# Weight differences of an fp32 encoder's MLPs by adding DMA transfers

## The chip, the cores and the metric

The kernel runs on one core of a Trainium2 chip. The metric is device time in microseconds (us); the median of three runs is compared. A core has TensorE (PE, with its weight loads as PEld), VectorE (DVE), ScalarE (ACT), GpSimd (POOL) and SyncE (SP), and 16 DMA engines that move data between HBM and SBUF.

## The reference

A two-layer encoder on x of shape (1, 512, 1024), all in float32. Layer 0 mixes tokens by dilated sliding-window attention, layer 1 by latent attention; each mixer is followed by an MLP with 4096 hidden columns:

```python
def sq_relu_mlp(h, w1, w2):
    a = jax.nn.relu(h @ w1)
    return (a * a) @ w2

def reference(x, ...):
    for i in range(DEPTH):
        h = rms_norm(x, norm_mix[i])
        ...
        x = x + y
        h = rms_norm(x, norm_ffn[i])
        x = x + sq_relu_mlp(h, ffn_w1[i], ffn_w2[i])
    return x
```

The change lies in the two MLPs alone.

## The kernel before

**Three passes for float32.** TensorE multiplies in the rounded format float32r. Each operand is split into a high part (its rounding) and a low part (the rest), and a product is summed from high x high, high x low and low x high. A weight unit is a tile of 128 partitions x 2 x 512 values (512 KB). `load_unit` brings it into `raw` by a DMA that SP issues, ScalarE copies it to `whi` (rounding it), and VectorE forms `wlo = raw - whi`. There are three buffers of `raw` and four each of `whi` and `wlo`, shared by everything that splits weights.

**The first matmul** (`up`) works in chunks of 1024 hidden columns, each in two groups of 512. A group has four units; each unit feeds 24 matmuls (2 slices of k, 4 output tiles `acc`, 3 passes). Then ScalarE evacuates each `acc` with a ReLU and squares it. The first group of a layer is special: it takes all four units at once and goes over the tokens in two halves.

**The second matmul** (`wino`, called by `down`) multiplies each chunk's 1024 x 1024 weight block with seven products of quarter blocks instead of eight, in the order 1, 5, 6, 3, 7, 2, 4. Each of the four quarters (b11, b12, b22, b21) is two units in `wqs`, loaded by SP. Some products need a difference of quarters: b11 is overwritten with b12 - b11 for product 5, then with b22 minus that for product 6, then with b21 minus that for product 4; b12 becomes b22 - b12 for product 7. `sub` does it, in two halves, on VectorE. Then `split_w` makes the high and low part as above, and 12 matmuls (PE tiles `sc` and `tp`) use each unit. VectorE also forms sums of activations (`stmp`) and adds the results to the residual stream (`add_to`). The last chunk of a layer goes another way (`down_last`).

**Order.** A layer runs up(0,0), up(0,1), then for each of three chunks up(ch+1,0), down(ch), up(ch+1,1), and down_last(3). Each engine has one instruction queue in fixed order, which a scheduler lays out when the program is built. Buffers come free by semaphores when their last reader is done.

Of the kernel before, what the change touches and what calls it, by code (L numbers as in the profile page):

```python
# [10 lines left out]
F32 = mybir.dt.float32  # L11
F32R = mybir.dt.float32r
AF = mybir.ActivationFunctionType
ALU = mybir.AluOpType
# [5 lines left out]
NT = S // P  # L20
# [67 lines left out]
def encoder_kernel(ctx: ExitStack, tc: tile.TileContext, x, norm_mix, norm_ffn, a_w_qkv, a_q_gain, a_k_gain,  # L88
                   a_w_o, b_w_in, b_q_a_gain, b_w_qb, b_kv_a_gain, b_w_kvb, b_q_gain, b_k_gain, b_w_o,
                   ffn_w1, ffn_w2, consts, out):  # L90
    nc = tc.nc
    V, A, G, PE = nc.vector, nc.scalar, nc.gpsimd, nc.tensor
    uid = [0]

    def nm(s):
        uid[0] += 1
        return f"{s}_{uid[0]}"
# [50 lines left out]
            nc.sync.dma_start(dst, src)  # L148
        return raw

    def load_unit(src, nk, dims, n, key=None, home=None):

        raw = early.pop(key) if key in early else load_raw(src, nk, dims, n)
        if home is None:
            home = [wp.tile([P, 2, 512], F32R, tag=t, name=nm(t)) for t in ("whi", "wlo")]
        hi, lo = home
        A.activation(hi[:, :nk, :n], raw[:, :nk, :n], AF.Copy)  # L157
        V.tensor_tensor(lo[:, :nk, :n], raw[:, :nk, :n], hi[:, :nk, :n].bitcast(F32), op=ALU.subtract)  # L158
        return hi, lo, nk

    def run_block(units, groups, n, mm, evac, outs=NT, name=None, halves=1):

        accs = [acc_p.tile([P, 512], F32, tag="acc", name=nm("acc")) for _ in range(outs)]
        total = sum(u[1] for u in units)
        ui = 0
        kt0 = 0  # L170
        for gi, g in enumerate(groups):
            loaded = []
            for _ in range(g):
                src, nk, dims = units[ui]
                loaded.append(load_unit(src, nk, dims, n, (name, ui)))
                ui += 1
            nkt = 0
            for hv in range(halves):
                for o in range(outs):
                    kt = kt0  # L180
                    for hi, lo, nk in loaded:
                        for j in range(nk):
                            for p_i, (lt, rt, oc) in enumerate(mm(o, kt, hi[:, j], lo[:, j], hv)):
                                PE.matmul(accs[o][:, oc], lhsT=lt, rhs=rt, start=(kt == 0 and p_i == 0 and hv == 0),  # L184
                                          stop=(kt == total - 1 and p_i == 2), skip_group_check=halves > 1)
# [303 lines left out]
    def wino(tag, Aq, w, wqs, pool, resid):  # L489

        v = w.rearrange("(k p) c -> p k c", p=P)
        raw, S = {}, {}

        def load(key, slot):
            ki, ni = key  # L500
            raw[key] = []
            for u in range(2):
                t = wqs[:, 2 * slot + u]
                k0 = 4 * ki + 2 * u
                nc.sync.dma_start(t, v[:, k0:k0 + 2, 512 * ni:512 * ni + 512])
                raw[key].append(t)
        for key, slot in zip(((0, 0), (0, 1), (1, 1), (1, 0)), SLOTS[tag % 2]):
            load(key, slot)
        b11, b12, b22, b21 = raw[0, 0], raw[0, 1], raw[1, 1], raw[1, 0]

        def sub(o, x, y):
            for u in range(2):
                V.tensor_tensor(o[u], x[u], y[u], op=ALU.subtract)  # L513

        def stmp(name, x, y, op):
            if name not in S:
                S[name] = pool.tile([P, 4, 256], F32, tag="S", name=nm("S"), bufs=2)
            V.tensor_tensor(S[name], x, y, op=op)

        def split_w(x):  # L520
            hi = wp.tile([P, 2, 512], F32R, tag="whi", name=nm("whi"))
            lo = wp.tile([P, 2, 512], F32R, tag="wlo", name=nm("wlo"))
            A.activation(hi, x, AF.Copy)  # L523
            V.tensor_tensor(lo, x, hi.bitcast(F32), op=ALU.subtract)  # L524
            return hi, lo

        def operands(p):
            if p == 1:
                return Aq(0, 0), b11
            if p == 5:  # L530
                stmp("c", Aq(1, 0), Aq(1, 1), ALU.add)
                sub(b11, b12, b11)
                return S["c"], b11
            if p == 6:
                stmp("c", S["c"], Aq(0, 0), ALU.subtract)
                sub(b11, b22, b11)
                return S["c"], b11
            if p == 3:
                stmp("c", Aq(0, 1), S["c"], ALU.subtract)
                return S["c"], b22  # L540
            if p == 7:
                stmp("d", Aq(0, 0), Aq(1, 0), ALU.subtract)
                sub(b12, b22, b12)
                return S["d"], b12
            if p == 2:
                return Aq(0, 1), b21
            sub(b11, b21, b11)
            return Aq(1, 1), b11

        def add_to(i, n, banks):  # L550
            for t in range(2):
                sl = resid[:, 2 * i + t, 512 * n:512 * n + 512]
                V.tensor_tensor(sl, sl, banks[t], op=ALU.add)

        banks = {}
        for p, chain, first, adds in ORDER:
            a, wq = operands(p)
            at = split_a(a, pool)
            if first:
                pl, tg = (sc_p, "sc") if chain == "a" else (tp_p, "tp")  # L560
                banks[chain] = [pl.tile([P, 512], F32, tag=tg, name=nm(tg)) for _ in range(2)]
            bk = banks[chain]
            for u in range(2):
                hi, lo = split_w(wq[u])
                for t in range(2):
                    for j in range(2):
                        k = 2 * u + j
                        ah = at[:, k, 0, t * P:(t + 1) * P]
                        al = at[:, k, 1, t * P:(t + 1) * P]
                        for i, (lt, rt) in enumerate(((ah, hi), (ah, lo), (al, hi))):  # L570
                            PE.matmul(bk[t], lhsT=lt, rhs=rt[:, j], start=(first and k == 0 and i == 0),  # L571
                                      stop=(k == 3 and i == 2), skip_group_check=True)
            for i, n in adds:
                add_to(i, n, bk)
# [6 lines left out]
    def mlp(layer, w1, w2, hT_m, resid, pool, done):  # L581
# [4 lines left out]
        def up(ch, grp):  # L586
# [6 lines left out]
            c0 = ch * 1024 + grp * 512  # L593
            first = c0 == 0
# [9 lines left out]
                A.activation(a2[:, f], acc, AF.Relu)  # L604
# [351 lines left out]
```

## Time and profile before

| | us |
|---|---|
| runs shown (3): lowest, median, highest | 1454.57, 1455.29, 1456.9 |
| profiled execution: its own time | 1457.98 |
| profiled execution: span | 1456.2 |
| PE busy in the span | 1422.8 |
| DVE busy | 903.5 |
| ACT busy | 710.3 |
| POOL busy | 117.4 |

A busy time is the sum of an engine's instructions, overlaps counted once. The engine whose share is highest need not be late everywhere: a wait matters where it stands in the chain that ended last. The profiled execution lies 2.7 us above the median. Rows of the profile name a line of the kernel, an engine, an operation, the tile written and the tiles read; the time in brackets is the engine's idle time just before, with what ended it.

### The profile page before, as it was taken

What the parts mean: (1) busy time and instruction counts of PE and PEld (TensorE: products, weight loads), DVE (VectorE), ACT (ScalarE), POOL (GpSimd) and SP (SyncE); (2) the same over time, 40 slices, a digit from 0 to 9 for tenths busy, and PEclk for the clock granted to TensorE, in tenths of its full rate; (3) what the DMA queues carried; (4) which work ended last, traced back from release to release, by engine and by line L of the source; (5) the groups of instructions that cost most, each with busy time, mean ns of one, the idle gap of its engine ahead of it and who ended that gap; (6) DMA issues with size and microseconds to landing.
All of it is one profiled execution on the core that took longest, in us unless ns stands there. A gap on an engine that the chain in (4) does not pass through costs nothing.

```text
span 1456.2 us, 19181 instructions
## 1 busy us (share of the span) xinstructions
PE 1422.8 (98%) x7164; PEld 1210.6 (83%) x7164; DVE 903.5 (62%) x1431; ACT 710.3 (49%) x1572; POOL 117.4 (8%) x133
## 2 busy tenths in 40 slices
PE   7999999999999999999999999999999999999998
PEld 6889889889988878888888888776778888888887
DVE  6765466556437655285776835688754286675832
ACT  5544455355335533553644543787633453544530
POOL 1120120011011100000000010322100000000000
PEclk9999999999999999999999999999999999999999
DMA  6325114322531334415151032300014305151031
GB/s 227 102 55 167 59 46 131 102 63 58 171 94 58 95 130 157 147 36 171 40 174 58 15 111 68 97 30 30 30 44 162 127 30 173 44 172 61 7 111 72
DMA packets 113053, 135.58 MB, mean 93 GB/s; under 512 B 7488, under 2 KB 72256, under 8 KB 112960
## 3 DMA queue, kind: packets, MB, share of 16 engines
q1 hardware_dynamic: 112960, 134.35, 29.5%
q8 instruction: 57, 0.93, 0.3%
q14 instruction: 36, 0.29, 0.1%
HBM read 130.13 MB, written 4.19 MB: 92 GB/s over the span
## 4 chain that ended last, share of the span: by engine, by line
PE 94%; ACT 3%; DVE 2%; issue 1%; DMA 0%; POOL 0%; SPq 0%; DVEq 0%; ACTq 0%
PE acc L184 64%; PE sc L571 9%; PE tp L571 7%; PE tp L123 4%; PE acc L867 1%; PE sc L761 1%; PE acc L843 1%; PE sco L440 1%; PE sco L444 1%; PE sc L351 1%; PE sc L843 1%; DVE wlo L158 1%; PE sc L344 0%; PE tp L867 0%; PE sc L340 0%
## 5 line engine op out<-in xcount | busy, mean ns | idle before, releaser
L184 PE MATMUL acc<-whi,hT 128*128 128x512 f32 (+2 forms) x1600 | 486.5, 379 | 5.5 <-DVE t L311 2.2
L158 DVE TENSOR_TENSOR wlo<-raw,whi 128x1024 fp32r<-128x1024 f32 (+3 forms) x186 | 215.3, 1162 | 297.5 <-ACT whi L157 296.5
L157 ACT ACTIVATE whi<-raw 128x1024 fp32r<-128x1024 f32 (+3 forms) x186 | 187.2, 1010 | 317.8 <-PE acc L184 256.6
L184 PEld LDWEIGHTS acc<-whi,hT 128*128 128x128 f32 x1600 | 296.3, 189 | 47.1 <-issue 2.9
L184 PE MATMUL acc<-hT_f,whi 128*128 128x512 f32 (+1 forms) x1152 | 322.7, 367 | 1.7 <-DVE resid L650 1.2
L184 PE MATMUL acc<-wlo,hT 128*128 128x512 f32 (+2 forms) x800 | 299.9, 375 | 0.0
L184 PEld LDWEIGHTS acc<-hT_f,whi 128*128 128x128 f32 x1152 | 209.1, 189 | 37.4 <-DVE resid L650 1.6
L184 PE MATMUL acc<-hT_f,wlo 128*128 128x512 f32 (+1 forms) x576 | 208.3, 366 | 0.0
L184 PEld LDWEIGHTS acc<-wlo,hT 128*128 128x128 f32 x800 | 151.3, 189 | 19.9 <-DVE wlo L158 0.5
L523 ACT ACTIVATE whi<-wqs 128x1024 fp32r<-128x1024 f32 x84 | 89.2, 1062 | 110.2 <-PE sc L571 42.6
L184 PEld LDWEIGHTS acc<-hT_f,wlo 128*128 128x128 f32 x576 | 109.0, 189 | 17.5
L571 PE MATMUL sc<-whi,asp 128*128 128x512 f32 x384 | 122.1, 389 | 0.0
L524 DVE TENSOR_TENSOR wlo<-wqs,whi 128x1024 fp32r<-128x1024 f32 x84 | 102.6, 1222 | 25.9 <-ACT whi L523 25.8
L131 POOL TENSOR_TENSOR qrs<-rs_v,nhalf 128x4 f32<-128x4 f32 x48 | 61.5, 1290 | 408.3 <-DVE rs_v L128 393.8
L571 PE MATMUL tp<-whi,asp 128*128 128x512 f32 x288 | 91.6, 389 | 0.0
L571 PEld LDWEIGHTS sc<-whi,asp 128*128 128x128 f32 x384 | 72.1, 188 | 14.9
L184 PE MATMUL acc<-whi,asp 128*128 128x512 f32 x256 | 78.9, 389 | 0.0
L571 PE MATMUL sc<-wlo,asp 128*128 128x512 f32 x192 | 74.7, 389 | 0.0
L571 PEld LDWEIGHTS tp<-whi,asp 128*128 128x128 f32 x288 | 54.0, 188 | 11.2
L136 ACT ACTIVATE junk<-acc 128x128 f32<-128x128 f32 x192 | 53.0, 276 | 18.9 <-PE acc L184 13.9
L513 DVE TENSOR_TENSOR wqs<-wqs 128x1024 f32<-128x1024 f32 x48 | 58.0, 1219 | 0.2
L184 PEld LDWEIGHTS acc<-whi,asp 128*128 128x128 f32 x256 | 48.1, 188 | 10.0
(191 smaller groups left out, 1895.4 us busy)
## 6 DMA issues: line engine op xcount, KB each, us to landing
raw<-in_ffn_w_dram SPq DMA_DIRECT2D x80, 512.0 KB, 3.7
raw<-in_a_w_qkv_dram SPq DMA_DIRECT2D x96, 256.0 KB, 3.4
wqs<-in_ffn_w_dram SPq DMA_DIRECT2D x48, 512.0 KB, 4.4
raw<-in_a_w_qkv_dram SPq DMA_DIRECT2D x64, 192.0 KB, 2.8
raw<-in_a_w_o_dram SPq DMA_DIRECT2D x8, 512.0 KB, 4.1
raw<-in_b_w_o_dram SPq DMA_DIRECT2D x8, 512.0 KB, 3.7
xt<-in_x_dram SPq DMA_DIRECT2D x8, 256.0 KB, 5.6
vd<-vt SPq DMA_DIRECT2D x8, 256.0 KB, 3.5
```

What stands on the lines that cost most here:

```text
L123: PE.transpose(o, i, ident)
L131: G.tensor_tensor(out, v[:, :n], nhalf[:, :n], op=ALU.pow)
L136: A.activation(junk, x, AF.Square, scale=1.0 / math.sqrt(dim), accum_out=out)
L157: A.activation(hi[:, :nk, :n], raw[:, :nk, :n], AF.Copy)
L158: V.tensor_tensor(lo[:, :nk, :n], raw[:, :nk, :n], hi[:, :nk, :n].bitcast(F32), op=ALU.subtract)
L184: PE.matmul(accs[o][:, oc], lhsT=lt, rhs=rt, start=(kt == 0 and p_i == 0 and hv == 0), stop=(kt == total - 1 and p_i == 2), skip_group_che ...
L351: PE.matmul(sc[:, r * P:(r + 1) * P], lhsT=qT[:, r * P:(r + 1) * P], rhs=kT[:, r * P:(r + 1) * P], start=True, stop=True)
L513: V.tensor_tensor(o[u], x[u], y[u], op=ALU.subtract)
L523: A.activation(hi, x, AF.Copy)
L524: V.tensor_tensor(lo, x, hi.bitcast(F32), op=ALU.subtract)
L571: PE.matmul(bk[t], lhsT=lt, rhs=rt[:, j], start=(first and k == 0 and i == 0), stop=(k == 3 and i == 2), skip_group_check=True)
L843: PE.matmul(sc, lhsT=lt, rhs=rt, start=(i == 0), stop=(i == 4))
```

## The change

Two computations of VectorE are given to the DMA engines. For the low part of the first matmul's weights (all groups but the first of each layer), ScalarE writes -whi into `wlo`, and POOL issues a DMA that reads the weights a second time from HBM and adds them into `wlo`. For a difference of quarter blocks, ScalarE writes -y in place, and a DMA of POOL adds x from HBM. The low parts of `split_w` stay on VectorE.

```diff
-    def load_unit(src, nk, dims, n, key=None, home=None):
+    def load_unit(src, nk, dims, n, key=None, home=None, by_dma=False):
...
         A.activation(hi[:, :nk, :n], raw[:, :nk, :n], AF.Copy)
-        V.tensor_tensor(lo[:, :nk, :n], raw[:, :nk, :n], hi[:, :nk, :n].bitcast(F32), op=ALU.subtract)
+        if by_dma:
+
+            A.activation(lo[:, :nk, :n], hi[:, :nk, :n].bitcast(F32), AF.Copy, scale=-1.0)
+            nc.gpsimd.dma_start(lo[:, :nk, :n], src, accum_op=ALU.add)
+        else:
+            V.tensor_tensor(lo[:, :nk, :n], raw[:, :nk, :n], hi[:, :nk, :n].bitcast(F32), op=ALU.subtract)
         return hi, lo, nk
...
         def sub(o, x, y):
+
+            ki, ni = x
             for u in range(2):
-                V.tensor_tensor(o[u], x[u], y[u], op=ALU.subtract)
+                k0 = 4 * ki + 2 * u
+                A.activation(o[u], y[u], AF.Copy, scale=-1.0)
+                nc.gpsimd.dma_start(o[u], v[:, k0:k0 + 2, 512 * ni:512 * ni + 512], accum_op=ALU.add)
...
-                sub(b11, b12, b11)
+                sub(b11, (0, 1), b11)
...
-            run_block(w_units(w1, c0, 512), [4] if first else [1] * 4, 512, mm, evac, halves=2 if first else 1)
+            run_block(w_units(w1, c0, 512), [4] if first else [1] * 4, 512, mm, evac, halves=2 if first else 1,
+                      by_dma=not first)
```

The other three calls of `sub` change like the one shown, and `run_block` hands `by_dma` on. Outside the two MLPs the order of the instructions stays as it was. Within them it moves, and three places matter.

ScalarE at the start of up(0,1), the first group with added low parts (`acc_5339` and `acc_5340` belong to up(0,0); `whi_5571` is up(0,1)'s first unit). Before:

```order
L604 ACTIVATE a_956_5336<-acc_5339 128x512 [waits PE_49]
L157 ACTIVATE whi_5571<-raw_5569 128x1024 [waits DMAHW0_49,PE_49]
L605 ACTIVATE a_956_5336<-a_956_5336 128x512 [waits Activation_49]
L157 ACTIVATE whi_5601<-raw_5599 128x1024 [waits DMAHW2_49,PE_49]
L157 ACTIVATE whi_5631<-raw_5629 128x1024 [waits DMAHW0_49,PE_49]
L604 ACTIVATE a_956_5336<-acc_5340 128x512 [waits PE_49]
```

After:

```order
L613 ACTIVATE a_956_5336<-acc_5339 128x512 [waits PE_49]
L157 ACTIVATE whi_5571<-raw_5569 128x1024 [waits DMAHW0_49,PE_49]
L614 ACTIVATE a_956_5336<-a_956_5336 128x512 [waits Activation_49]
L157 ACTIVATE whi_5602<-raw_5600 128x1024 [waits DMAHW2_49,PE_49]
L160 ACTIVATE wlo_5572<-whi_5571 128x1024 [waits Activation_49]
L157 ACTIVATE whi_5633<-raw_5631 128x1024 [waits DMAHW0_49,PE_49]
L613 ACTIVATE a_956_5336<-acc_5340 128x512 [waits PE_49]
L160 ACTIVATE wlo_5603<-whi_5602 128x1024 [waits Activation_49]
```

The negation of the first unit (L160) now stands behind the second unit's high part, and its transfer can be issued only after it.

ScalarE at the start of down(0): the high parts of product 5 (`whi_5886`, `whi_5902` before; `whi_5896`, `whi_5912` after) and of product 6 (`whi_5926`, `whi_5942` before; `whi_5938`, `whi_5954` after), among the evacuations of up(1,0). Before:

```order
L523 ACTIVATE whi_5886<-wqs_5335 128x1024 [waits PE_49]
L604 ACTIVATE a_989_5697<-acc_5698 128x512 [waits PE_49]
L605 ACTIVATE a_989_5697<-a_989_5697 128x512 [waits Activation_49]
L604 ACTIVATE a_989_5697<-acc_5699 128x512 [waits PE_49]
L605 ACTIVATE a_989_5697<-a_989_5697 128x512 [waits Activation_49]
L604 ACTIVATE a_989_5697<-acc_5700 128x512 [waits PE_49]
L605 ACTIVATE a_989_5697<-a_989_5697 128x512 [waits Activation_49]
L523 ACTIVATE whi_5902<-wqs_5335 128x1024 [waits DVE_49,PE_49]
L604 ACTIVATE a_989_5697<-acc_5701 128x512 [waits PE_49]
L605 ACTIVATE a_989_5697<-a_989_5697 128x512 [waits Activation_49]
L523 ACTIVATE whi_5926<-wqs_5335 128x1024 [waits DVE_49,PE_49]
L523 ACTIVATE whi_5942<-wqs_5335 128x1024 [waits DVE_49,PE_49]
```

After:

```order
L532 ACTIVATE whi_5896<-wqs_5335 128x1024 [waits DMASW2_49,PE_49]
L613 ACTIVATE a_989_5701<-acc_5702 128x512 [waits PE_49]
L614 ACTIVATE a_989_5701<-a_989_5701 128x512 [waits Activation_49]
L521 ACTIVATE wqs_5335<-wqs_5335 128x1024 [waits DVE_49]
L613 ACTIVATE a_989_5701<-acc_5703 128x512 [waits PE_49]
L613 ACTIVATE a_989_5701<-acc_5704 128x512 [waits PE_49]
L614 ACTIVATE a_989_5701<-a_989_5701 128x512 [waits Activation_49] x2
L532 ACTIVATE whi_5912<-wqs_5335 128x1024 [waits DMASW3_49,PE_49]
L613 ACTIVATE a_989_5701<-acc_5705 128x512 [waits PE_49]
L614 ACTIVATE a_989_5701<-a_989_5701 128x512 [waits Activation_49]
L532 ACTIVATE whi_5938<-wqs_5335 128x1024 [waits DMASW4_49,PE_49]
L521 ACTIVATE wqs_5335<-wqs_5335 128x1024 [waits DVE_49] x2
```

The high parts now wait for adding transfers (DMASW) where they waited for VectorE, and the negations (L521) of product 6's halves stand between them: each waits for the low part of product 5 on VectorE, and holds what is behind it.

TensorE at the start of up(1,1), behind the last product of down(0) (`wlo_6124` before and `wlo_6140` after are its first unit's low part). Before:

```order
L571 MATMUL sc_5842<-whi_6099,asp_6080 128x512
L184 MATMUL acc_6117<-hT_f_4965,whi_6123 128x512 [waits Activation_49]
L184 MATMUL acc_6117<-hT_f_4965,whi_6123 128x512
L184 MATMUL acc_6117<-hT_f_4965,wlo_6124 128x512 [waits DVE_49]
L184 MATMUL acc_6117<-hT_f_4965,whi_6123 128x512 x2
```

After:

```order
L580 MATMUL sc_5850<-whi_6115,asp_6096 128x512
L189 MATMUL acc_6133<-hT_f_4965,whi_6139 128x512 [waits Activation_49]
L189 MATMUL acc_6133<-hT_f_4965,whi_6139 128x512
L189 MATMUL acc_6134<-hT_f_4965,whi_6139 128x512 x2
L189 MATMUL acc_6135<-hT_f_4965,whi_6139 128x512 x2
L189 MATMUL acc_6136<-hT_f_4965,whi_6139 128x512 x2
L189 MATMUL acc_6133<-hT_f_4965,wlo_6140 128x512 [waits DMASW2_49]
```

Eight matmuls on the high part now stand ahead of the first one that needs the low part, and that one waits for an adding transfer. up(0,1) begins in the same way. In a block, three matmuls on high parts are pulled ahead of the low part of product 6's second half.

More of the change, by code (lines that the diff above doesn't have):

```diff
@@ L157, in load_unit, with run_block @@
         A.activation(hi[:, :nk, :n], raw[:, :nk, :n], AF.Copy)
-        V.tensor_tensor(lo[:, :nk, :n], raw[:, :nk, :n], hi[:, :nk, :n].bitcast(F32), op=ALU.subtract)
+        if by_dma:
[3 more added lines that the diff above has]
+            V.tensor_tensor(lo[:, :nk, :n], raw[:, :nk, :n], hi[:, :nk, :n].bitcast(F32), op=ALU.subtract)
         return hi, lo, nk
-    def run_block(units, groups, n, mm, evac, outs=NT, name=None, halves=1):
+    def run_block(units, groups, n, mm, evac, outs=NT, name=None, halves=1, by_dma=False):
         accs = [acc_p.tile([P, 512], F32, tag="acc", name=nm("acc")) for _ in range(outs)]
@@ L174, in run_block @@
                 src, nk, dims = units[ui]
-                loaded.append(load_unit(src, nk, dims, n, (name, ui)))
+                loaded.append(load_unit(src, nk, dims, n, (name, ui), by_dma=by_dma))
                 ui += 1
@@ L535, in operands @@
                 stmp("c", S["c"], Aq(0, 0), ALU.subtract)
-                sub(b11, b22, b11)
+                sub(b11, (1, 1), b11)
                 return S["c"], b11
@@ L546, in operands @@
                 return Aq(0, 1), b21
-            sub(b11, b21, b11)
+            sub(b11, (1, 0), b11)
             return Aq(1, 1), b11
```

2 lines of the change are left out of this document (1 added, 1 removed).

## The prediction

> **What bounds the kernel now.** I read the page's busy times and the chain that ended last first, since they say whose time counts; then stretches of the first MLP; then single instructions at the places where the change could make TensorE wait. From the page:
>
> ```profile
> span 1456.2 us, 19181 instructions
> PE 1422.8 (98%) x7164; PEld 1210.6 (83%) x7164; DVE 903.5 (62%) x1431; ACT 710.3 (49%) x1572; POOL 117.4 (8%) x133
> PE 94%; ACT 3%; DVE 2%; issue 1%; DMA 0%; POOL 0%; SPq 0%; DVEq 0%; ACTq 0%
> ```
>
> TensorE is the bound; VectorE, which the change relieves, carries 2% of the chain. Where is that 2%? The stretches of the first MLP (columns: length, then busy of PE, PEld, DVE, ACT, POOL, granted clock, share of the DMA engines, GB/s), in order two first-matmul groups, one seven-product block of the second matmul, two more groups:
>
> ```profile
> 595.00:638.64 43.64, 43.64 (x194) 36.13 (x194) 27.20 (x24) 23.53 (x31) 0.00 (x0) 1.00 0.31 96
> 638.64:676.72 38.08, 38.08 (x170) 31.53 (x169) 32.28 (x34) 19.62 (x20) 0.00 (x0) 1.00 0.45 138
> 676.72:720.24 43.52, 43.52 (x194) 36.04 (x193) 24.28 (x22) 20.03 (x26) 0.00 (x0) 1.00 0.25 73
> ```
>
> In each, PE's busy time equals the length: not one idle moment where the change acts. VectorE is loaded (32.3 of 38.1 us) but never late. So nothing can be won there, and the question is only which of the new transfers come too late.
>
> **What is removed and added.** Per instruction, from the page's groups:
>
> ```profile
> L158 DVE TENSOR_TENSOR wlo<-raw,whi 128x1024 fp32r<-128x1024 f32 (+3 forms) x186 | 215.3, 1162 | 297.5 <-ACT whi L157 296.5
> L157 ACT ACTIVATE whi<-raw 128x1024 fp32r<-128x1024 f32 (+3 forms) x186 | 187.2, 1010 | 317.8 <-PE acc L184 256.6
> L523 ACT ACTIVATE whi<-wqs 128x1024 fp32r<-128x1024 f32 x84 | 89.2, 1062 | 110.2 <-PE sc L571 42.6
> L524 DVE TENSOR_TENSOR wlo<-wqs,whi 128x1024 fp32r<-128x1024 f32 x84 | 102.6, 1222 | 25.9 <-ACT whi L523 25.8
> L131 POOL TENSOR_TENSOR qrs<-rs_v,nhalf 128x4 f32<-128x4 f32 x48 | 61.5, 1290 | 408.3 <-DVE rs_v L128 393.8
> L513 DVE TENSOR_TENSOR wqs<-wqs 128x1024 f32<-128x1024 f32 x48 | 58.0, 1219 | 0.2
> ```
>
> Low parts: 56 units (7 of 8 column groups, 4 units, 2 layers); sums of blocks: 48. VectorE loses 56 x 1.16 + 48 x 1.22 = 124 us, worth nothing by the stretches. ScalarE gains 104 negated copies at 1.06 = 110 us; one period of two groups and a block (81.6 us) holds 16 of them, so its busy time there goes from 20.0 + 19.6 to 56.6 us: covered as work, not as order. POOL gains 104 adding transfers of 512 KB. POOL has 0.00 busy in these stretches, so nothing else queues there; but each transfer stands in POOL's order, and TensorE or ScalarE now waits for its landing.
>
> **The unknown: L, from a transfer's issue on POOL to its landing.** No row of before shows an adding transfer, nor one that POOL issues. The nearest are SP's plain loads (last number: median us to landing):
>
> ```profile
> raw<-in_ffn_w_dram SPq DMA_DIRECT2D x80, 512.0 KB, 3.7
> wqs<-in_ffn_w_dram SPq DMA_DIRECT2D x48, 512.0 KB, 4.4
> L505 SPq DMA_DIRECT2D wqs<-in_ffn_w_dram x8: 417/568/1051, 567.6 to 574.6; - x8
> DMA to landing us min/median/max: 5.6/10.3/11.7
> 571.00:578.00 7.00, 7.00 (x62) 7.00 (x61) 3.91 (x6) 3.75 (x6) 0.55 (x1) 1.00 1.04 382
> ```
>
> The same bytes alone take 3.7 us; inside a burst that keeps all DMA engines busy (382 GB/s, so 524 KB / 382 = 1.37 us a transfer) they take 10.3. These are the ends: 3.7 and 10.3. I stay near the lone load, because the adds fall where the share is 0.25 to 0.45, and add two things: the old contents have to be read beside the source, 1.37 more; and POOL's smallest instruction takes 1.29 where SP's issue inside the 3.7 takes about 0.4, 0.9 more. L = 6.0.
>
> The Trainium skill, in DMA: Bandwidth & Descriptors, under the anatomy of one DMA on the gpsimd path, fits 2.0 us plus bytes over 436 GB/s to plain transfers of POOL; my estimate from it is 3.2 us, by which the sum below would be 9.4 instead of 19.8. The lone load of SP already takes 3.7 here, so I keep the rows.
>
> **Term 1, the second column group of each layer.** The first group holds all four buffers of high and low parts to its end. ScalarE and PE there:
>
> ```profile
> 592.85 1.06 ACT L157 ACTIVATE whi<-raw 128x1024 fp32r<-128x1024 f32 x1
> 594.34 1.99 ACT L157 ACTIVATE whi<-raw 128x1024 fp32r<-128x1024 f32 x2
> 594.93 1.55 PE L184 MATMUL acc<-hT_f,whi 128*128 128x512 f32 x6
> 638.64 5.44 PE sc L571 x24
> ```
>
> The high part is made at 592.85, the next two from 594.34 on (two in 1.99, so the second unit's until 595.35); in the new order the negation comes behind the latter and ends at 596.4. PE starts the group at 594.93 with eight matmuls on the high part (5.44 / 24 = 0.227 each) and needs the low part at 596.74. It lands at 596.4 + L and some 0.1 for semaphores: PE stands for L - 0.2 = 5.8 us. Later units of the group are asked for 5.44 us apart and are covered. After such a stand the clock drops; stretches of 1 us around a gap of before:
>
> ```profile
> 1116.37 1.11 PE L123 MATMUL tp<-ck,xn 128*128 128x128 f32 x4 [1.35 <-DVE hT_f L221]
> 1115.00:1116.00 1.00, 0.02 (x1) 0.00 (x0) 1.00 (x2) 0.76 (x2) 0.00 (x0) 0.92 0.97 371
> 1116.00:1117.00 1.00, 0.63 (x3) 0.64 (x4) 0.97 (x3) 0.00 (x0) 0.00 (x0) 0.50 1.04 403
> 1118.00:1119.00 1.00, 1.00 (x7) 1.00 (x7) 1.00 (x2) 0.12 (x1) 0.00 (x0) 0.50 0.99 332
> 1119.00:1120.00 1.00, 1.00 (x9) 1.00 (x9) 0.52 (x1) 0.88 (x1) 0.00 (x0) 0.88 0.97 281
> ```
>
> From 1116 to 1119 it is 0.50: 0.08 + 3 x 0.50 + 0.12 = 1.7 us lost. Two layers: 2 x (5.8 + 1.7) = 15.0.
>
> **Term 2, the chain of sums in a seven-product block.** Block b11 is rewritten for product 5, then from that for product 6, in place: negate, add, split, negate, add, split. ScalarE's order decides, since the negations stand between the squared-ReLU evacuations of the group before:
>
> ```profile
> 625.04 1.23 DVE L524 TENSOR_TENSOR wlo<-wqs,whi 128x1024 fp32r<-128x1024 f32 x1 [1.24 <-ACT whi L523]
> 633.01 1.06 ACT L523 ACTIVATE whi<-wqs 128x1024 fp32r<-128x1024 f32 x1 [2.24 <-PE acc L184]
> 634.60 0.60 ACT L604 ACTIVATE a<-acc 128x512 f32<-128x512 f32 x1 [0.53 <-PE acc L184]
> 637.32 0.60 ACT L604 ACTIVATE a<-acc 128x512 f32<-128x512 f32 x1
> 639.43 0.58 ACT L604 ACTIVATE a<-acc 128x512 f32<-128x512 f32 x1
> ```
>
> Product 1's first low part is ready at 626.27, so product 5's sum is negated by 627.35 and lands at 627.4 + L = 633.4, beside the buffer, which PE frees at 633.0. Product 5's high part is then made by 634.5; behind it stand one evacuation (0.60), its square (0.63), the low part (until 635.7, on VectorE) and the negation for product 6's first half (1.06), which with the semaphores between ends at 637.2. Its sum lands L later; then high part 1.06, the negation of the second half 1.05, its transfer L, high part 1.06, low part 1.22 on VectorE, with 0.1 for semaphores. PE wants that low part at 638.64 + 5 x 2.72 + 3 x 0.227 = 652.92 (five units of 12 matmuls, three hoisted ones). Late by 637.2 + 2L + 4.5 - 652.9 = 2L - 11.2 = 0.8 us; free below L = 5.6. Six blocks: 4.8, without a clock drop, as the gap is shorter than the 1.35 above. Products 7 and 4 have longer: 7's block is negated a block ahead, 4's has four products' time.
>
> **Term 3, the first group after a block.**
>
> ```profile
> 668.60 1.06 ACT L157 ACTIVATE whi<-raw 128x1024 fp32r<-128x1024 f32 x1 [1.66 <-PE tp L571]
> 676.72 43.52 PE acc L184 x192
> 569.05 0.56 SPq L505 DMA_DIRECT2D wqs<-in_ffn_w_dram  x1
> 586.49 0.60 ACT L604 ACTIVATE a<-acc 128x512 f32<-128x512 f32 x1 [7.43 <-PE acc L184]
> ```
>
> The buffer comes free at 668.6; high part and negation end at 670.8; PE wants the low part eight matmuls into the group, 676.72 + 1.8 = 678.5. So L up to 7.6 is free; here next-block loads share the engines, one of them ahead adds 1.4: 7.4. Free. Other units have 16.3 us from buffer to use: free. Two early negations stand between the last norm evacuations of each layer and wait for loads (at most 569.05 + 11.7 = 580.8); what they hold back is not wanted before the first group's second half, 24 matmuls of 0.12 ahead of the evacuation at 586.49, so at 583.6: free.
>
> Sum: 15.0 + 4.8 + 0 = 19.8 us. The profiled execution took 1458.0 (span 1456.2), 2.7 above the median of 1455.3; I carry the 19.8 to the median: **1475 us**.
>
> **Rivals.**
> - *The DMA engines become the bound.* A period moves 16 plain loads (16 x 1.37 = 22 us); 16 adds at twice a load cost 44 more: 66 of 81.6. At three times 88, at four times 110: 6 to 28 us more in each of six periods, on top of term 1 and more of term 2. Time: 1520 to 1640. Against it: share 0.31 at most in a group. The Trainium skill, Collectives: The Full Stack, on the bandwidth ceiling, says that adding halves the rate because two sources are read on one ring; by that this rival falls away. No run here shows it yet. 0.13.
> - *ScalarE waits for loads.* The negations for the next block's product 7 stand ahead of the splits of products 2 and 4. With loads landing in 4.4 us they fit; at the burst's 10.3 the split comes 3.5 us late, six times: 1455 + 15 + 5 + 21 = 1496. 0.08.
> - *Not slower.* The stall of term 1 vanishes if L is below about 0.2, and is within the noise (0.2%, 2.9 us, is what a measurement of this kernel can tell from no change) if L stays below 1.6, the place being the second group alone. The smallest load, 32 KB, takes 2.2 us, so this needs a transfer faster than any seen: 1455 to 1458. Shares of VectorE gained elsewhere cannot pay for it, as the stretches had no idle PE. 0.06.
> - *As summed*, late transfers at terms 1 to 3: 0.73, its own range 1462 (L = 3.7: 2 x 3.5, no clock drop) to 1514 (L = 7.5: 2 x 9.0, and 6 x (3.8 + 1.7) + 6 x 1.3 = 41).
>
> Range for 8 in 10: 1462 to 1535. It takes in the loads' rival and the milder end of the DMA rival; its top is term 1 to 3 at L = 8.4 (2 x 9.9 + 6 x 7.3 + 6 x 2.2 = 77). At L = 10.3 it would be 1570, which is left to the 2 in 10. Faster 0.02, same 0.04, slower 0.94.
>
> **What would show it.** Right: PE idle of some 6 us at the start of each layer's second group, released by a DMA into wlo, and the clock at 0.50 after it; PE or VectorE waiting in blocks around product 6's second half; VectorE near 780 us, ScalarE near 820, 104 transfers of POOL landing in about 6 us. Wrong: L far from 6.0, which moves term 2 twice as fast as L in each of six blocks; or DMA shares near 1 through whole groups.

## The result, and the profile after

The changed kernel takes 1532.64 us (median of 4 runs, 1529.61 to 1534.93) against 1455.18 us: a ratio of 1.0529 with a 95% interval of 1.0507 to 1.0551, 77 us slower. In what follows a stand is a wait of TensorE between two matmuls, a landing is the time from the issue of a transfer until its data are in place, and the first unit of a group is the first of its four weight units. Lines of the changed kernel's page, in the order of those shown of before (busy times; the chain that ended last; the DMA queues with packets, MB and share of the 16 engines; DMA issues with the median us to landing):

```profile
span 1532.1 us, 19476 instructions
PE 1443.2 (94%) x7164; PEld 1216.7 (79%) x7164; DVE 781.8 (51%) x1327; ACT 804.6 (53%) x1676; POOL 242.7 (16%) x237
PE 69%; issue 12%; DMA 10%; ACT 5%; DVE 3%; POOL 2%; SPq 0%; POOLq 0%; ACTq 0%; DVEq 0%
q1 hardware_dynamic: 112960, 134.35, 27.5%
q0 software_dynamic: 28288, 54.53, 21.2%
raw<-in_ffn_w_dram SPq DMA_DIRECT2D x80, 512.0 KB, 5.8
wlo<-in_ffn_w_dram POOLq DMA_DIRECT2D x56, 512.0 KB, 9.5
wqs<-in_ffn_w_dram SPq DMA_DIRECT2D x48, 512.0 KB, 7.1
wqs<-in_ffn_w_dram POOLq DMA_DIRECT2D x48, 512.0 KB, 6.5
```

VectorE and ScalarE are where they were forecast (781.8 and 804.6 us). TensorE has the same 7164 matmuls, is busy 20.4 us longer (most of it by a lower clock) and idle for the rest. The plain loads, too, now take longer to land: 5.8 and 7.1 us where they took 3.7 and 4.4. The same stretch of the first MLP, before and then after (columns as in the prediction; the second last is the share of the DMA engines):

```profile
595.00:890.00 295.00, 295.00 (x1303) 244.27 (x1303) 191.00 (x185) 139.66 (x160) 7.18 (x9) 1.00 0.30 93
```

```profile
595.00:890.00 295.00, 268.27 (x1141) 217.93 (x1141) 118.78 (x121) 169.62 (x192) 60.11 (x50) 0.96 0.77 168
```

Where TensorE stood, from the timeline of after (start, busy, instruction, in brackets the idle time ahead of it and what ended it): the second group of each layer, product 6 in the first block of each layer, and the groups behind the first two blocks.

```profile
596.13 0.73 PE L189 MATMUL acc<-hT_f,whi 128*128 128x512 f32 x2 [1.32 <-ACT a L613]
605.33 0.79 PE L189 MATMUL acc<-hT_f,wlo 128*128 128x512 f32 x1 [8.47 <-DMA wlo<-in_ffn_w_dram]
664.78 0.73 PE L580 MATMUL sc<-whi,asp 128*128 128x512 f32 x2 [1.98 <-ACT whi L532]
696.71 0.80 PE L189 MATMUL acc<-hT_f,wlo 128*128 128x512 f32 x1 [4.78 <-DMA wlo<-in_ffn_w_dram]
788.50 0.79 PE L189 MATMUL acc<-hT_f,wlo 128*128 128x512 f32 x1 [4.30 <-DMA wlo<-in_ffn_w_dram]
1189.00 0.80 PE L189 MATMUL acc<-hT_f,wlo 128*128 128x512 f32 x1 [8.23 <-DMA wlo<-in_ffn_w_dram]
1250.17 0.73 PE L580 MATMUL sc<-whi,asp 128*128 128x512 f32 x2 [3.67 <-ACT whi L532]
```

The transfer behind the stand of 8.47 us, from the chain of waits (issue, landing):

```profile
594.95 10.34 DMA wlo<-in_ffn_w_dram
```

All stands of over 0.2 us in the two MLPs from the second groups on add up to 53.2 us: 19.3 at the two second groups, 15.6 at product 6 (six blocks), 16.7 in the first unit behind a block (4.78, 4.30, 0.75, 3.73, 3.10, none), 1.6 in later units. With the 20.4 us of longer busy time that is 73.6 of the 75.9 us between the two spans. So the slowdown came and was almost four times the forecast one. It came at the second groups and at product 6, which the forecast had charged, and behind the blocks, which it had called free.

### The profile page after: what moved, and what is told of

It reads as the page before. It is cut to its first block, busy times and chain, and to the rows that moved or that the text cites. A ratio compares the mean times of both kernels' runs of the same rounds, so it can differ in the third digit from the quotient of the medians.

```text
span 1532.1 us, 19476 instructions
## 1 busy us (share of the span) xinstructions
PE 1443.2 (94%) x7164; PEld 1216.7 (79%) x7164; DVE 781.8 (51%) x1327; ACT 804.6 (53%) x1676; POOL 242.7 (16%) x237
## 3 DMA queue, kind: packets, MB, share of 16 engines
q1 hardware_dynamic: 112960, 134.35, 27.5%
q0 software_dynamic: 28288, 54.53, 21.2%
## 4 chain that ended last, share of the span: by engine, by line
PE 69%; issue 12%; DMA 10%; ACT 5%; DVE 3%; POOL 2%; SPq 0%; POOLq 0%; ACTq 0%; DVEq 0%
PE acc L189 52%; DMA wlo<-in_ffn_w_dram 5%; DMA wqs<-in_ffn_w_dram 4%; PE tp L123 4%; PE tp L580 2%; PE sc L580 2%; POOL wqs L522 1%; PE acc L877 1%; PE acc L853 1%; ACT whi L532 1%; PE sc L771 1%; DVE wlo L533 1%; PE sco L449 1%; PE sco L445 1%; PE sc L356 1%
## 5 line engine op out<-in xcount | busy, mean ns | idle before, releaser
L189 PE MATMUL acc<-hT_f,whi 128*128 128x512 f32 (+1 forms) x1152 | 327.9, 374 | 4.3 <-ACT a L613 2.6
L189 PEld LDWEIGHTS acc<-hT_f,whi 128*128 128x128 f32 x1152 | 214.4, 194 | 42.3 <-ACT a L613 3.5
L189 PE MATMUL acc<-hT_f,wlo 128*128 128x512 f32 (+1 forms) x576 | 214.5, 382 | 35.2 <-DMA wlo<-in_ffn_w_dram 35.0
L163 DVE TENSOR_TENSOR wlo<-raw,whi 128x1024 fp32r<-128x1024 f32 (+3 forms) x130 | 146.8, 1134 | 161.5 <-ACT whi L157 160.7
L189 PEld LDWEIGHTS acc<-hT_f,wlo 128*128 128x128 f32 x576 | 113.8, 198 | 58.8 <-DMA wlo<-in_ffn_w_dram 40.1
L580 PE MATMUL sc<-whi,asp 128*128 128x512 f32 x384 | 125.6, 396 | 14.5 <-ACT whi L532 14.5
L161 POOL DMA_DIRECT2D wlo<-in_ffn_w_dram x56 | 67.3, 1203 | 239.8 <-ACT wlo L160 186.0
L527 DVE TENSOR_TENSOR S<-a 128x1024 f32<-128x1024 f32 x12 | 14.2, 1222 | 177.5 <-ACT a L614 177.5
L522 POOL DMA_DIRECT2D wqs<-in_ffn_w_dram x48 | 58.0, 1209 | 252.6 <-ACT wqs L521 247.0
L521 ACT ACTIVATE wqs<-wqs 128x1024 f32<-128x1024 f32 x48 | 50.7, 1056 | 34.3 <-DMA wqs<-in_ffn_w_dram 28.9
```

What stands on the lines that cost most here:

```text
L161: nc.gpsimd.dma_start(lo[:, :nk, :n], src, accum_op=ALU.add)
L521: A.activation(o[u], y[u], AF.Copy, scale=-1.0)
L522: nc.gpsimd.dma_start(o[u], v[:, k0:k0 + 2, 512 * ni:512 * ni + 512], accum_op=ALU.add)
```

## Experiments

The main theory was that an adding transfer lands in some 6.4 us when alone and 8 to 10 beside others, and that TensorE stands where it is wanted sooner. The rivals were the engine time of 104 additions, ScalarE's order, and POOL's route itself. The code cuts are against the changed kernel, and `...` stands for lines or words left out; each experiment's interval is its ratio to before.

**The two halves.** *low_only* keeps the added low parts and puts the sums back on VectorE; *sums_only* keeps the added sums and puts the low parts back:

```
-                A.activation(o[u], y[u], AF.Copy, scale=-1.0)
-                nc.gpsimd.dma_start(o[u], v[:, k0:k0 + 2, ...], accum_op=ALU.add)
+                V.tensor_tensor(o[u], raw[x][u], y[u], op=ALU.subtract)
```

> Only the low parts of the first matmul's weights go by adding transfers; the sums of blocks are back on VectorE. Theory (each transfer lands some 6.4 us after its issue when alone and 8 to 10 us beside others, and TensorE waits where it is wanted sooner): the stand at the second group of each layer stays, 2 x 9.7 us and about 2 x 5 of clock; product 6 no longer waits; the first group after a block waits 0 to 4 us, six times, less than now since no sum shares the engines: 1485 to 1505. Rival (the adds together fill the DMA engines, and it is their number that counts): with 56 of 104 adds left, none of them overlapping a sum, little over the stand itself: 1470 to 1480, with the stand below 7 us. Rival (ScalarE's order, split and negated sums in front of evacuations): the low parts are not the trouble, below 1470.

```
-                      by_dma=not first)
+                      by_dma=False)
```

> Only the sums of blocks go by adding transfers; the low parts are back on VectorE. Theory of landing times: late by 2L - 11.2 at product 6, with the lone L of 6.4 1.6 us, with 7 to 7.5 of a shared engine 3 to 4 us, six times, no or little clock lost: 1465 to 1480; no stand at the second group or behind a block. If low_only and sums_only add up to the 77 us of the full change, the two halves do not hinder each other; if their sum is below 60, the rest is contention between them. Rival (number of adds): 1456 to 1460.

Measured: 1489.36 us (1.0223, 1.0208 to 1.0238) and 1477.94 us (1.0148, 1.0133 to 1.0163), 33 and 22 us more than before. That is 55 of 77: some 22 us appear only when both halves are there. Low parts alone: the chain of waits behind the first block, and the stand that it ended:

```profile
679.74 9.31 DMA wlo<-in_ffn_w_dram
689.09 0.50 PE L189 MATMUL acc<-hT_f,wlo 128*128 128x512 f32 x1 [1.87 <-DMA wlo<-in_ffn_w_dram]
```

TensorE wanted this part at 689.09 - 1.87 = 687.2, 7.5 us after the issue: the free time that the prediction had worked out (7.6). The landing took 9.31. In the full kernel the same issue came later, because ScalarE stood in the block; its timeline, then the transfer of the first unit in the chain:

```profile
678.25 1.06 ACT L521 ACTIVATE wqs<-wqs 128x1024 f32<-128x1024 f32 x1 [5.93 <-DMA wqs<-in_ffn_w_dram]
685.03 1.07 ACT L160 ACTIVATE wlo<-whi 128x1024 fp32r<-128x1024 f32 x1
686.40 10.27 DMA wlo<-in_ffn_w_dram
```

The negation at 678.25 waited 5.93 us for a load of the next block, and the first unit's split and negation were in the queue behind it. Of the 7.5 us before TensorE's need (696.71 - 4.78 = 691.93) 5.5 were left, and the landing took 10.27: 2.0 + 1.0 us more than with low parts alone. This is how the halves hinder each other here, and the other blocks show the same. In the four blocks that have a next one in their layer, the negation waited 5.93, 6.08, 5.7 and 5.03 us for a next-block load, and the first unit's transfer was issued 5.5, 5.4, 6.0 and 6.6 us ahead of the need; in all six blocks of *low_only* it was 7.5. The four landings took 9.6 to 10.3 us (8.6 to 9.5 in the same blocks of *low_only*). In the two blocks without a next one 7.5 us were left, and the stands were 0.75 us and none. All stands of the two halves add up to 38.0 us, those of the full change to 53.2; 9.6 of the 15.2 us between them lie behind the blocks. In each of the four blocks with a next one the later issue is the larger part.

With sums alone, TensorE stood 1.76 to 2.07 us at product 6 in each of the six blocks.

**The first unit of each late group on VectorE** (*unit0_dve*):

```
-                loaded.append(load_unit(src, nk, dims, n, (name, ui), by_dma=by_dma))
+                loaded.append(load_unit(src, nk, dims, n, (name, ui), by_dma=by_dma > (ui == 0)))
...
-                      by_dma=not first)
+                      by_dma=0 if first else 2 - grp)
```

> The full change, but the first of the four units of every second column group (the group at each layer's start and those behind a block) has its low part made by VectorE. Theory of landing times: the second unit is wanted 5.4 us later, so stands of 9.7 us at the second group shrink to 0 to 4, those behind a block vanish, with them most of the clock loss; product 6's waits of 2.2 to 3.9 stay: 1470 to 1485. Rival (DMA engines full in the groups): the stand only moves to the second unit, which shares the same engines: above 1505.

Measured: 1504.85 us (1.0322, 1.0298 to 1.0346), next to the rival's bound and far from the theory's 1485. The long stands went, but shorter ones came in the units behind:

```profile
602.16 0.79 PE L189 MATMUL acc<-hT_f,wlo 128*128 128x512 f32 x1 [2.34 <-DMA wlo<-in_ffn_w_dram]
1273.87 0.50 PE L189 MATMUL acc<-hT_f,wlo 128*128 128x512 f32 x1 [2.97 <-DMA wlo<-in_ffn_w_dram]
```

Stands add up to 30.6 us (15.1 at product 6, 15.5 at low parts in 11 places). My expectation that only the first units were late was wrong. The transfer behind the stand of 2.97 us was issued late, because ScalarE had waited 9.80 us for the plain load of its unit; the share of the DMA engines was 0.96 there. With nearly all additions left, the engines are at times too full for later units as well.

**The same transfers without the addition** (*plain*): `accum_op=ALU.add` is taken away in both places, so the low parts and the differences are not formed.

> The full change with all 104 transfers of POOL as plain ones: they overwrite what ScalarE negated instead of adding to it, same bytes, same queue, same order; left out is the addition. If the addition is what is dear (old contents read and written, so about twice the engines' time): landing near 4.5 to 5 us, stand at the second group 4 to 6 us, product 6 free, nothing behind a block: 1463 to 1475, and POOL's queue takes near 12% of the engines instead of 21%. If it is POOL's route and issue of 1.2 us that is dear, landing stays at 6 to 10 us: above 1505.

Measured: 1479.66 us (1.0156, 1.0141 to 1.0171), some 5 us above the expected range: the group behind the second block of each layer still stood 0.92 and 2.87 us, and the second groups 4.53 and 6.16. From its page:

```profile
q0 software_dynamic: 22144, 54.53, 12.4%
wlo<-in_ffn_w_dram POOLq DMA_DIRECT2D x56, 512.0 KB, 5.6
wqs<-in_ffn_w_dram POOLq DMA_DIRECT2D x48, 512.0 KB, 4.2
```

The same bytes on the same queue hold the engines for 12.4% of 1478 us instead of 21.2% of 1532: the addition takes 1.77 times as much engine time, and 2.3 us longer to land (6.5 against 4.2 for the sums). So 53 of the 77 us belong to the addition, 24 to moving the work to a negation and a transfer of POOL at all.

**One addition for each layer** (*one_add*): sums on VectorE as in *low_only*, and of the low parts only the first unit of the second group.

```
+                loaded.append(load_unit(src, nk, dims, n, (name, ui), by_dma=by_dma and ui == 0))
...
+                      by_dma=ch == 0 and grp == 1)
```

> Two adding transfers in all: the low part of the first unit of each layer's second group; everything else is on VectorE as before. It measures one landing that meets no other addition. If it is the additions of the next units that lengthen this landing from the lone 6.4 us to about 10: a stand of 6 to 6.5 us, and 1.3 ahead of it (evacuation behind the negation), about 2 us of clock: 2 x 9.5, 1474 to 1477. If it is the plain loads that share the engines there: a stand of 7.7 as with all low parts added, 1.3 ahead of it and 4 of clock: 1480 to 1484.

Measured: 1477.03 us (1.0146, 1.0131 to 1.0161). The time lies at the edge of the first explanation, but the stand and the landing speak for the second, the plain loads: with no other addition anywhere near, this one took 9.2 us. What shared the engines was four plain loads. The stand, and the DMA issues between 590 and 606 us:

```profile
602.75 0.80 PE L189 MATMUL acc<-hT_f,wlo 128*128 128x512 f32 x1 [7.41 <-DMA wlo<-in_ffn_w_dram]
raw<-in_ffn_w_dram SPq DMA_DIRECT2D x4, 512.0 KB, 5.5
wlo<-in_ffn_w_dram POOLq DMA_DIRECT2D x1, 512.0 KB, 9.2
```

**The same with thin loads** (*few_loads*): those four loads bring an eighth of their columns.

```
+            w = 64 if thin else n
+            nc.sync.dma_start(dst[:, :, :w], src[:, :, :w])
+            if thin:
+                V.memset(raw[:, :, 64:], 0.0)
...
+                      thin={(0, 1): (3,), (1, 0): (0, 1, 2)}.get((ch, grp), ()))
```

> One adding transfer in each layer as in the run before with one addition (stand 7.4 us, landing 9.2), but the four plain loads of 512 KB that are issued within 7 us around it are cut to an eighth of their columns (left out: the other columns of these units, which VectorE sets to zero). If the loads lengthen the landing: 6.3 to 6.6 us, a stand of 4.7 to 5, and less clock lost: 1469 to 1473. If the landing is long for another reason (the first transfer after 22 idle us on POOL, its issue of 1.35 us): 9 us and 1477 again.

Measured: 1470.73 us (1.0105, 1.009 to 1.0121). The stand, and the landing of the one transfer in its place in the first layer:

```profile
601.35 0.79 PE L192 MATMUL acc<-hT_f,wlo 128*128 128x512 f32 x1 [4.26 <-DMA wlo<-in_ffn_w_dram]
DMA to landing us min/median/max: 6.1/6.1/6.1
```

So the plain loads are what made 6.1 into 9.2 us at the second group; with the other additions the full change took 10.34. The loads were in the trace of before; its windows of 2 us there (the group's mean was 0.31):

```profile
596.00:598.00 2.00, 2.00 (x11) 1.65 (x10) 1.77 (x2) 1.94 (x4) 0.00 (x0) 1.00 0.78 232
598.00:600.00 2.00, 2.00 (x11) 1.65 (x10) 1.23 (x1) 1.51 (x2) 0.00 (x0) 1.00 0.84 252
600.00:602.00 2.00, 2.00 (x11) 1.65 (x10) 1.23 (x1) 0.12 (x1) 0.00 (x0) 1.00 0.81 295
```

The Trainium skill, DMA: Bandwidth & Descriptors, in the section on queues, rings and completion order, says that each engine takes the queues it has work for in turn, a packet from each. The two runs are in keeping with that, though they do not show the turns: the addition's 512 KB landed 3.1 us later with some 2 MB of loads in the other queue.

**Sources in SBUF** (*from_sbuf*): the additions read the copy that is there already (`raw[:, :nk, :n]`, `raw[x][u]`) in place of HBM.

> The full change, but each addition reads its source from the copy that is already in SBUF instead of from HBM again; the slot of that copy is held until the addition lands. If the second read of HBM is what makes an addition long: landing 4.5 to 5.5 us, 1475 to 1495. If it is the addition itself (old contents read, two packets' work for one): landing as in the full change, 6.4 alone and 9 to 10 beside others, and with a raw slot held longer the loads behind it are later: 1525 to 1550.

Measured: 1496.13 us (1.0278, 1.0252 to 1.0304), 1 us above the first range. A sum lands in 4.6 us, and TensorE no longer stood at product 6 in any block; most of the rest came from the slot of the raw copy, which is held until the addition lands (the next run tests this), as evacuations came late behind waiting splits. Two lines of the page and one of the timeline:

```profile
wqs<-wqs POOLq DMA_DIRECT2D x48, 512.0 KB, 4.6
q0 software_dynamic: 14976, 54.53, 19.8%
797.03 1.22 PE L189 MATMUL acc<-hT_f,whi 128*128 128x512 f32 x2 [4.47 <-ACT a L613]
```

With the source in HBM a sum thus lands some 1.8 us later, but takes little more of the engines' time (19.8% of 1496 us is 296, against 325 of the full change). The packets are fewer, too (14976 against 28288), and no run separates the two.

**The same with free slots** (*from_hi*): the low parts add `hi` in place of `raw`, and so come out as zero.

> As the run with sources in SBUF, but the low parts' additions read the rounded high part instead of the raw copy (left out: the low parts come out as zero), so the slot of the raw copy is free as early as in the full change. If holding that slot was what delayed loads and evacuations there (18 us of waits for evacuations): these waits go, but the four loads share the engines with the first addition again; landing there 6.5 to 7.5 instead of 5, stand 4.5 to 5.5 and 1.3 ahead of it; product 6 free, as sums land in 4.6 which is below the 5.6 of the prediction: 1468 to 1478. If evacuations are late for ScalarE's order: above 1485.

Measured: 1477.35 us (1.0153, 1.0138 to 1.0168). The waits for evacuations went, but for the 1.32 us at each second group, so the others came from the held slot. The stands for the low part at the second groups were 6.27 and 5.52 us, up to 0.8 longer than expected.

**Negations on VectorE**, for all 104 (*neg_dve*) and for the sums alone (*sums_neg_dve*):

```
-                A.activation(o[u], y[u], AF.Copy, scale=-1.0)
+                V.tensor_scalar(o[u], y[u], -1.0, None, op0=ALU.mult)
```

> The full change, but the 104 negated copies are made by VectorE instead of ScalarE; the transfers are the same. Theory of landing times: term by term the same stands, less the 1.3 us at the second group (evacuations no longer behind a negation) and some 0.5 to 1 us less at product 6 and at the second group, as the next units' splits are not behind negations: 1515 to 1530. Rival (ScalarE's order is what makes product 6 and the groups late): product 6 free and stands halved: 1485 to 1500.

> The sums alone by adding transfers from HBM, as in sums_only (1478), but negated by VectorE. If product 6 is late because each negation waits in ScalarE's order behind evacuations and splits, on top of two landings: no stand, 1455 to 1459. If two landings of 6.4 us are enough by themselves: 1470 to 1478.

Measured: 1507.57 us (1.0357, 1.0342 to 1.0373), between the two ranges, and 1458.35 us (1.0014, 1.0004 to 1.0023). With the sums alone they land as late as in *sums_only* (6.4 against 6.5 us), yet no high part of product 6 is waited for; new with the sums alone are two waits for VectorE's additions to the residual, 0.44 and 0.97 us. With the sums alone, ScalarE's and POOL's timelines around product 6's second half, negated by ScalarE (*sums_only*):

```profile
637.90 1.06 ACT L532 ACTIVATE whi<-wqs 128x1024 fp32r<-128x1024 f32 x1
642.56 1.06 ACT L532 ACTIVATE whi<-wqs 128x1024 fp32r<-128x1024 f32 x1 [2.45 <-PE sc L580]
643.52 1.04 ACT L521 ACTIVATE wqs<-wqs 128x1024 f32<-128x1024 f32 x1
644.87 1.20 POOL L522 DMA_DIRECT2D wqs<-in_ffn_w_dram  x1 [7.37 <-ACT wqs L521]
```

and by VectorE (*sums_neg_dve*):

```profile
640.03 0.69 DVE L521 TENSOR_SCALAR wqs<-wqs 128x1024 f32<-128x1024 f32 x1
641.03 1.20 POOL L522 DMA_DIRECT2D wqs<-in_ffn_w_dram  x1 [3.20 <-DVE wqs L521]
```

The negation needs the low part of the split at 637.90. On ScalarE it stood behind the split of product 6's first half, which itself waited; on VectorE it follows that low part at once, and its transfer is issued 3.8 us sooner. What is late at product 6 is therefore the landing and ScalarE's order together: either a landing of 4.6 us or a free engine for the negation removes the stand. With all 104, the second groups still stood 6.73 and 6.88 us for their low part: at the second groups ScalarE's order had been worth only some 2.5 us for each layer. The groups behind blocks stood up to 4.85 us, no less than in the full change. There VectorE's order made the negation as late as ScalarE's had; behind the first block (the transfer, then the stand):

```profile
680.99 10.10 DMA wlo<-in_ffn_w_dram
691.12 0.50 PE L189 MATMUL acc<-hT_f,wlo 128*128 128x512 f32 x1 [4.85 <-DMA wlo<-in_ffn_w_dram]
```

The need was at 691.12 - 4.85 = 686.27, so 5.3 us were left for a landing of 10.10.

**Only where there is time** (*slack*): 48 additions, the low parts of up(1,0), up(2,0) and up(3,0) and the sums of products 7 and 4. *sbuf_sums*: 72, the same low parts and all sums, their sources in SBUF.

```
+                if x in ((0, 1),) or (x == (1, 1) and o is b11):
+                    V.tensor_tensor(o[u], raw[x][u], y[u], op=ALU.subtract)
+                    continue
...
-                      by_dma=not first)
+                      by_dma=grp == 0 and ch > 0)
```

> 48 of the 104 adding transfers, only where no stand was seen: low parts of the first column group of each later hidden block (24), and the sums of products 7 and 4 (24); the second groups, and the sums of products 5 and 6, are on VectorE. Theory (a landing that is late for a reader costs, the number of additions does not): no stand of TensorE, 1455 to 1459. Rival (engine time of the additions, 0.74 us of the 77 for each): 48 x 0.74 = 36 us more, 1485 to 1495.

> 72 of the 104 adding transfers: all 48 sums, with their sources in SBUF, and the low parts of the first column group of each later hidden block, from HBM; the second groups are on VectorE. By the prediction's working for product 6 (late by 2L - 11.2) and the 4.6 us that such a sum took, no stand: 1455 to 1458. Rival (product 6 was free only because TensorE stood elsewhere and gave it time): stands of 1 to 2 us in six blocks, 1463 to 1470.

Measured: 1455.71 us (1.0001, 0.9991 to 1.0010) and 1456.33 us (1.0003, 0.9994 to 1.0012), without one stand of over 0.2 us from the second groups of the MLPs on. Busy times of the latter:

```profile
PE 1419.4 (98%) x7164; PEld 1206.8 (83%) x7164; DVE 820.1 (56%) x1359; ACT 774.7 (53%) x1644; POOL 188.1 (13%) x205
```

So it is not the number of additions, up to 72, that costs, but those that are late. VectorE is relieved by 83 us and the time is the same. No version beat the kernel before.

## Why the prediction was right or wrong

Right: the direction, the bound (nothing to win from VectorE: *sbuf_sums* relieved it by 83 us for nothing), two of the three kinds of places, and the working of the orders. The rule for product 6, late by 2L - 11.2, gives 1.6 us for the lone landing of 6.4; *sums_only* stood 1.76 to 2.07. Its free point of 5.6 fits *sbuf_sums* (4.6 us, no stand), but it holds for ScalarE's order alone: with the negation on VectorE there was no stand at 6.4 either. The lone L was nearly right, too: 6.0 forecast, 6.1 to 6.5 seen. That was in part luck, as its two additions to SP's 3.7 erred in opposite directions: POOL's plain sums landed in 4.2, so 0.5 and not 0.9, and the addition made 6.5 of it, so 2.3 and not 1.37. The engine time of the rival's first price, twice a load, was right: an addition takes 1.90 times a load's per byte (21.2% for 54.53 MB against 27.5% for 134.35). The Trainium skill, Collectives: The Full Stack, gives half the rate for adding in a collective, in its part on the bandwidth ceiling; the 1.90 here agrees with it.

Wrong: the sum, 1475 us, by 58. The terms, forecast against the profiled run:

| term | forecast, us | measured, us |
|---|---|---|
| 1: stand at the second groups | 2 x 5.8 | 9.79 + 9.55 |
| 1: clock after it | 2 x 1.7 | about 2 x 2.0 |
| 2: product 6 | 6 x 0.8 | 15.6 |
| 3: first unit behind a block | 0 | 16.7 |
| later units | 0 | 1.6 |
| clock after the other stands | 0 | about 12.7 |
| rest of the longer busy time | 0 | about 3.7, not placed |

- The step that failed first is the choice of one L. "I stay near the lone load, because the adds fall where the share is 0.25 to 0.45": these were means over 40 us. The additions are issued when a buffer comes free, and so are the plain loads; in the 6 us around the first one the share was 0.78 to 0.84 already in before, and *few_loads* shows that these loads alone are worth 3.1 us of landing, and the first transfer of the full change took 10.34. Nor is the share of before the one that counts: the prediction's own rival had the engines busy for 66 of 81.6 us, 0.81, with the additions in (0.77 measured), and this was not carried back into L.
- Term 3 failed by its second assumption as well, that the first unit is asked for as early as in before. The second rival, ScalarE waiting for a next-block load, was real (5.93 us at 678.25, 5.0 to 6.1 in four blocks) and was paid there, not at the splits of products 2 and 4 where it was priced.
- Term 2 was forecast at 0.8 us a block; the lone L of 6.4 makes it 1.6, and sharing the engines made it up to 3.67 in the full kernel. That it rises twice as fast as L was in the list of what would make the forecast wrong.
- Term 1's working held. An evacuation behind the negation comes 1.32 us later, which it left out, but TensorE would have stood for the landing in that time anyway: both waits together are the landing less some 0.5 us, whatever it is (9.79 at 10.34, 8.73 at 9.25 in *one_add*, 5.58 at 6.1 in *few_loads*), where the forecast took 0.2 off. Only L was wrong.
- The clock was charged at the second groups only. After 605.33 it was 0.50 to some 609, 2.0 us lost, near the 1.7 forecast. But it fell after shorter stands, too: the stretches after the 3.67 us at product 6,

```profile
1250.00:1251.00 1.00, 0.73 (x2) 0.30 (x2) 0.85 (x1) 1.00 (x3) 0.00 (x0) 0.99 0.75 135
1251.00:1252.00 1.00, 0.88 (x2) 0.86 (x3) 1.00 (x2) 1.00 (x3) 0.00 (x0) 0.50 0.03 4
1254.00:1255.00 1.00, 1.00 (x5) 0.81 (x4) 1.00 (x2) 0.86 (x1) 0.79 (x1) 0.80 0.80 272
```

and the same after 1.87 us in *low_only*. At 0.50 TensorE was busy for 7.9 us behind the two stands at the second groups and for 25.4 us behind six others. Half of that is lost, 4.0 and 12.7 us; the remaining 3.7 of the 20.4 are not explained by the clock.

The rival of full DMA engines is half right: they are not the bound over a period (*slack* and *sbuf_sums* with 48 and 72 additions cost nothing), but with 96 or 104 they are full enough that units with 16 us of time come late now and then (1 to 3 us in *unit0_dve*, where a load of their own landed late). The time lies where that rival put it, 1520 at least, for a mixture of causes. It also lies inside the forecast range, near its top, and that is in part luck: the top took one L of 8.4 everywhere, some 20, 44 and 13 us for terms 1 to 3, where 23, 19 and 26 were measured with their clock. In the rival called not slower, the smallest load is misread: loads of 0.5 KB are in before as well, at 5.6 to 6.1 us. The 2.2 us is the shortest landing of a load, so that argument stands.

Open: how the 22 us between the halves divide between the engines' load and ScalarE's wait was read from issues and landings block by block, not from a run of its own. 2.3 us of the difference of the spans and 3.7 us of TensorE's longer busy time are not placed.

## What to carry to other kernels

Price a new transfer by what shares the DMA engines in the microseconds after its issue, with the new transfers counted in, and not by a mean over the stage: buffers that come free start loads and additions at the same moment. Before moving work from an idle-enough engine to a transfer, list for each use the time between its issue and its need; where that is above the shared landing the move costs nothing, and where it is not, a stand is paid by itself and, when it leaves TensorE idle for about 2 us of one 3.41 us step of the clock (below), a second time by half the rate after it. If the engine relieved was not the bound, nothing is won even then.

## What the runs showed of the hardware

- An adding transfer of 512 KB from HBM issued by POOL landed in 6.1 us beside four loads of 64 KB (*few_loads*) and in 9.2 beside four of 512 KB (*one_add*). The medians of the sums were 6.4 and 6.5 us with the sums alone (*sums_neg_dve*, *sums_only*), 4.6 from SBUF (*from_sbuf*) and 4.2 plain from HBM (*plain*). POOL's issue took 1.20 us for adding from HBM, 0.72 for plain, 0.87 for adding from SBUF.
- With the source in HBM and not in SBUF the landing was 1.8 us longer, for 10% more engine time; the addition itself held the engines 1.77 times as long as a plain copy on the same queue.
- Whether TensorE's clock halves after a stand depends on where the stand falls on a fixed grid of 3.41 us. In the changed kernel's trace the clock falls at 599.04, 694.62, 786.78 and 1250.99, which are 28, 27 and 136 steps of 3.413 us apart, and the low stretches in the MLPs last one, two or three steps (3.41, 6.82, 10.24 us). The 1.87 us in *low_only* fell within one step, the 1.98 us at 664.78 across the edge of two. The two steps, first of *low_only* and then of the changed kernel, each with the one behind it:

```profile
686.36:689.77 3.41, 1.54 (x7) 0.95 (x6) 0.00 (x0) 1.21 (x2) 1.23 (x2) 1.00 1.05 231
689.77:693.18 3.41, 3.41 (x10) 2.64 (x9) 0.00 (x0) 0.00 (x0) 0.00 (x0) 0.50 1.10 262
660.49:663.90 3.41, 2.32 (x11) 1.58 (x9) 0.87 (x2) 0.22 (x1) 0.00 (x0) 1.00 1.09 191
663.90:667.31 3.41, 2.31 (x9) 1.55 (x10) 2.54 (x3) 3.41 (x4) 0.00 (x0) 1.00 0.56 103
```

  On the grids of all fourteen traces, from 30 us on to the end of the work, each step at full clock in which TensorE was idle for 1.96 us or more was followed by 0.50, none with less than 1.54 was, and between the two both happened. The Trainium skill, TensorE: Matmul & The Clock Gate, Part 1, puts the clock at half rate after at least one idle window of about 3.4 us and lets these windows run freely. The half rate, the length and the free running agree; that a window a little over half idle is enough is what the measurement adds.
- A negated copy of 128 x 1024 float32 in place took 0.69 us on VectorE and 1.06 on ScalarE.
